# Low parts of the key tiles copied in turns of their own, and the last products all on VectorE: a two-layer decoder trunk on one Trainium2 core

## The chip, the cores and the metric

The kernel runs on one core of one Trainium2 chip. The metric is the device time of one execution in microseconds (us); the time of a kernel is the median over runs. TensorE does the matrix products; VectorE (DVE), ScalarE (ACT) and GpSimd (POOL) do elementwise work; SyncE (SP) issues the loads and stores. PE, DVE, ACT, POOL and SP are the names in the rows.

## The reference

Two layers of a decoder trunk run for 1024 prompt positions and for 8 samples of one position each, with shared weights. Cut to what matters here:

```
# layer 0: gated DeltaNet heads and an RG-LRU beside them -> out projection -> residual
# layer 1: sliding-window attention (16 query heads, 4 key heads of 64, window 128) -> out projection -> residual
# each layer: RMSNorm -> SwiGLU FFN (2816) -> residual; one RMSNorm at the end
def window_attend(qg, kk, vv, rel, keep, sinks, slopes):
    s = einsum('bqhgd,bkhd->bhgqk', qg, kk) * SWA_HEAD_DIM ** -0.5
    s = where(keep, s - slopes * rel, -inf)
    m = maximum(max(s, -1), sink)
    p = exp(s - m)
    p = p / (sum(p, -1) + exp(sink - m))
    return einsum('bhgqk,bkhd->bqhgd', p, vv)
...
y = rmsnorm(x, norm_final)        # x * rsqrt(mean(x*x)) * w, the last thing computed
```

## The kernel before

Activations are kept transposed, the model's channels on the 128 partitions, the positions along a row; the 1024 prompt positions and the 8 samples are cut into two halves of 512 and 520 columns (`t` = 0, 1). Every product with a weight is made of three products of rounded numbers: a value is split into a high part (rounded) and a low part (value less high part); `wh` and `wl` are the two parts of a weight tile, loaded to `raw`, rounded on ACT and subtracted on DVE.

Attention of layer 1: a key tile `k` holds two key heads (p = 0, 1), one on partitions 0 to 63, one on 64 to 127. `ev_k` takes the projected keys out of PSUM and starts the coroutine `co_k(p, t, k)`. For the scores each head's keys must lie on both partition halves. So `co_k` makes, for each half s: the high part in its own half (ACT, in `stack`), the low part by a subtraction (POOL), and the copy of each to the other half (ACT). The four tiles `kf[p]` are the high parts of the two heads (0 and 1) and their low parts (2 and 3). Of (p0, t0) these are s_12462, s_12463, s_12464, s_12465, of (p1, t0) s_12780, s_12781, s_12782, s_12783, in this order. `ready.add(("kf", p, t))` then lets the attention groups `co_att(j, t, q)` start that need it: scores (128x256 products), masked maximum on DVE, exponentials on ACT, scalings on DVE and POOL (`TENSOR_SCALAR s<-s,mx`), transposes on PE through PSUM (`MATMUL PS<-con,s` of 128x128), their evacuation on ACT (`COPY s<-PS`), products with the values (PV, `att_pv`). All this is side work. The main work is the stream of weight products: q, k and v projections, then the output projection (out1), half by half. PSUM is cut into main banks for the weight products and a ring of four side banks (`sd()`) that transposes, scores and PV products take in turn. The eight samples have an attention of their own, `co_att_s`, whose cached keys are loaded while out1 runs. `ev_out` empties out1's banks on DVE and makes the squares for the next norm; `co_blocks` computes that norm from sums of squares on PE.

The order on every engine is fixed when the program is built. The class `Sched` keeps a clock for each engine with estimated costs; each call goes through `Sched.call` (line 237, which is why all rows show L237), and side work is a list of generators that the planner runs between the main products when it believes that they can go on. In a generator `yield "ACT"` means "go on when ACT is believed free", `yield 0` "go on when what I issued is believed done", `yield` of a function "go on when it is true".

`co_final` closes the kernel: for each of three column pieces (432, 344, 256 wide) it computes the final norm's factor `r` and multiplies eight tiles by it, two per output tile, then issues the store. In the last piece (`last`) the eight products are spread over two engines.

Of the kernel before, what the change touches and what calls it, by code (L numbers as in the profile page):

```python
# [321 lines left out]
def trunk_kernel(ctx: ExitStack, tc: tile.TileContext, xT, consts, small, wba, win, lruw, wout0, wqkv, wout1, wgu, wdn,  # L322
# [10 lines left out]
    V, A, G, T, SP, SPA = (S.wrap(n, e) for n, e in (  # L333
        ("DVE", nc.vector), ("ACT", nc.scalar), ("POOL", nc.gpsimd), ("PE", nc.tensor), ("SP", nc.sync),
        ("SPA", nc.scalar)))
# [24 lines left out]
    def alloc(dt=F32):  # L360
        wait_free()
        t, i = new_slot(dt)
        return Buf(t, i, None, dt)
# [12 lines left out]
    def free(*bs):  # L376
        for b in bs:
            if b.half is None:
                free_slots.append(b.slot)
                continue  # L380
            halves[b.dt].append(b)
            owner[b.slot] += 1
            if owner[b.slot] == 2:
                halves[b.dt][:] = [x for x in halves[b.dt] if x.slot != b.slot]
                free_slots.append(b.slot)
# [60 lines left out]
    def split(ap, n):  # L446
        return ap.rearrange("p (c n) -> p c n", c=n)
# [298 lines left out]
    with tc.manual_schedule():  # L746
# [703 lines left out]
        for t in range(2):  # L1450
            gx = half_x(xs0, t)
            for n, w in enumerate((ORDER_0, ORDER_1)[t].split()):
                i = int(w[1])
# [176 lines left out]
        def ffn(layer, wn, dst, sqs, final):  # L1630
# [178 lines left out]
            def ev_last(m, o, w):  # L1809
                def e(ps, full):  # L1810
                    xt = xr[m].a[:, o:o + w]
                    V.tensor_tensor(out=xt, in0=ps[:, 0], in1=xt, op=ALU.add)
                    if m == 0:
                        fin[o] = tuple(halloc().a[:, 0:w] for _ in range(4))
                    q, q7, r, tmp = fin[o]
                    if m < 7:
                        sum_sq(xt, q, m, tmp, G)
                    else:
                        A.activation(out=q7, in_=xt, func=AF.Square)
                        S.spawn(co_final(o, w, [q, q7], r), 0)[0] = S.ready([q, q7], False)  # L1820
                    A.activation(out=xt, in_=xt, func=AF.Identity, scale=sv("nfin", m, 1))
                return e

            def co_final(o, w, qs, r):
                yield from co_norm(qs, w, r, True)
                last = o + w == W
                for m0 in range(0, 8, 2):
                    yb = alloc()
                    y = split(yb.a[:, 0:2 * w], 2)
                    if not last:  # L1830
                        yield "DVE"
                    for i in range(2):
                        (G if last and m0 + i in (3, 5, 7) else V).tensor_tensor(
                            out=y[:, i], in0=xr[m0 + i].a[:, o:o + w], in1=r, op=ALU.mult)
                    SP.dma_start(out=yT.rearrange("(m p) n -> p m n", m=8)[:, m0:m0 + 2, o:o + w], in_=y)
                    free(yb)
# [67 lines left out]
        def ev_k(p, t):  # L1904
            w = HWS[t]

            def f(ps, full):
                k = halloc()
                V.tensor_tensor(out=split(k.a[:, 0:w], 1 + t), in0=ps, in1=rhalf(t), op=ALU.mult)
                if t:  # L1910
                    SP.dma_start(out=p_kT[p * 128:p * 128 + 128, :], in_=k.a[:, 384:512])
                    G.tensor_copy(out=KN[:, 8 * p:8 * p + 8], in_=k.a[:, 512:520])
                else:
                    kf[p] = tuple(alloc(F32R) for _ in range(4))
                S.spawn(co_k(p, t, k), 0)
            return f

        def stack(src, dst, w, o=0):
            for s in range(2):
                a, b = (slice(64 * x, 64 * x + 64) for x in (s, 1 - s))  # L1920
                A.copy(out=dst[s].a[a, o:o + w], in_=src.a[a, 0:w])
                yield a, b, dst[s].a, src.a[a, 0:w], dst[s].a[a, o:o + w].bitcast(F32)

        def co_k(p, t, k):
            cols = slice(512 * t, 512 * t + 512)
            yield "ACT"
            for s, (a, b, hi, x, xh) in enumerate(stack(k, kf[p], 512, 512 * t)):
                kl = kf[p][2 + s].a
                G.tensor_tensor(out=kl[a, cols], in0=x, in1=xh, op=ALU.subtract)
                A.copy(out=hi[b, cols], in_=hi[a, cols].bitcast(F32))  # L1930
                A.copy(out=kl[b, cols], in_=kl[a, cols].bitcast(F32))
            ready.add(("kf", p, t))
            yield 0
            free(k)
# [363 lines left out]
        a, b = ph_in[1][:2]  # L2298
# [177 lines left out]
```

## Time and profile before

| | us |
|---|---|
| median of 3 runs | 2346.76 |
| the runs | 2352.08, 2346.25, 2346.76 |
| the profiled execution | 2351.13 |
| its span, first to last instruction | 2349.0 |
| TensorE busy | 2280.2 (97%) |
| VectorE, ScalarE, GpSimd busy | 1354.2, 989.1, 804.6 |
| mean granted clock of TensorE | 0.986 |

The profiled execution's own time is 2.1 us over its span. The busy times are of one execution; TensorE's clock has the levels 2.4 and 1.2 GHz (1.0 and 0.5 in the windows).

### The profile page before, as it was taken

What the parts mean: (1) busy time and instruction counts of PE and PEld (TensorE: products, weight loads), DVE (VectorE), ACT (ScalarE), POOL (GpSimd) and SP (SyncE); (2) the same over time, 40 slices, a digit from 0 to 9 for tenths busy, and PEclk for the clock granted to TensorE, in tenths of its full rate; (3) what the DMA queues carried; (4) which work ended last, traced back from release to release, by engine and by line L of the source; (5) the groups of instructions that cost most, each with busy time, mean ns of one, the idle gap of its engine ahead of it and who ended that gap; (6) DMA issues with size and microseconds to landing.
All of it is one profiled execution on the core that took longest, in us unless ns stands there. A gap on an engine that the chain in (4) does not pass through costs nothing.

```text
span 2349.0 us, 40227 instructions
## 1 busy us (share of the span) xinstructions
PE 2280.2 (97%) x15984; PEld 2121.2 (90%) x15984; DVE 1354.2 (58%) x2295; ACT 989.1 (42%) x2014; POOL 804.6 (34%) x748
## 2 busy tenths in 40 slices
PE   8899999899999999999999999899999999999998
PEld 6777999689899999999999798779899999999998
DVE  7887687566766665463236557565766544462334
ACT  6775676534522222241124677653522222241214
POOL 1533453332355554410002444431445544410003
PEclk9999999999999999999999999999999999999999
DMA  4332124234334432263213211444333222263222
GB/s 160 103 128 54 51 79 124 75 113 140 126 117 143 128 114 77 81 234 127 70 61 113 64 57 57 130 136 134 132 113 140 90 82 75 79 244 110 71 64 73
DMA packets 122236, 250.69 MB, mean 107 GB/s; under 512 B 24560, under 2 KB 50976, under 8 KB 122016
## 3 DMA queue, kind: packets, MB, share of 16 engines
q1 hardware_dynamic: 121760, 247.83, 32.1%
q8 instruction: 126, 2.06, 0.4%
q14 instruction: 62, 0.51, 0.1%
q10 hardware_dynamic: 288, 0.29, 0.0%
HBM read 199.26 MB, written 50.90 MB: 106 GB/s over the span
## 4 chain that ended last, share of the span: by engine, by line
PE 85%; DVE 6%; ACT 3%; issue 2%; POOL 1%; DMA 1%; SPq 0%; DVEq 0%; ACTq 0%; POOLq 0%
PE PS L237 85%; DVE s L237 4%; ACT s L237 2%; DVE wl L237 1%; POOL s L237 1%; ACT wh L237 1%; SPq L237 0%; ACT L237 0%; DMA s<-ckT 0%; DVE oss L237 0%; DMA pd<-s 0%; DMA s<-xT 0%; DMA lw<-lruw 0%; DMA d<-cm 0%; DVE mx L237 0%
## 5 line engine op out<-in xcount | busy, mean ns | idle before, releaser
L237 PE MATMUL PS<-s,wh 128*128 128x260 f32 (+4 forms) x7936 | 1597.4, 317 | 11.9 <-ACT s L237 6.8
L237 PEld LDWEIGHTS PS<-s,wh 128*128 128x128 f32 x7936 | 1225.0, 189 | 84.2 <-ACT s L237 8.6
L237 PE MATMUL PS<-s,wl 128*128 128x260 f32 (+4 forms) x3968 | 974.6, 317 | 1.6 <-DVE wl L237 1.5
L237 PEld LDWEIGHTS PS<-s,wl 128*128 128x128 f32 x3968 | 658.2, 190 | 34.8 <-DVE wl L237 2.0
L237 POOL TENSOR_TENSOR s<-s,s 128x520 f32<-128x520 f32 (+6 forms) x219 | 296.8, 1356 | 983.7 <-ACT s L237 908.8
L237 DVE TENSOR_TENSOR s<-PS,s 128x520 f32<-128x520 f32 (+7 forms) x430 | 294.0, 684 | 300.6 <-PE PS L237 294.4
L237 DVE TENSOR_TENSOR wl<-raw,wh 128x512 fp32r<-128x512 f32 (+1 forms) x327 | 272.8, 840 | 296.2 <-ACT wh L237 294.2
L237 ACT CAST wh<-raw 128x512 fp32r<-128x512 f32 x352 | 211.7, 608 | 367.6 <-PE PS L237 341.8
L237 PE MATMUL PS<-s,s 128*128 128x260 f32 (+12 forms) x2944 | 343.2, 288 | 9.3 <-ACT s L237 3.3
L237 PEld LDWEIGHTS PS<-s,s 128*128 128x128 f32 (+3 forms) x2944 | 302.4, 171 | 44.4 <-issue 17.0
L237 DVE TENSOR_TENSOR wl<-s,wh 128x512 fp32r<-128x512 f32 x208 | 194.4, 936 | 207.1 <-ACT wh L237 206.8
L237 ACT ACTIVATE s<-s 128x520 f32<-128x520 f32 (+5 forms) x197 | 123.0, 631 | 244.0 <-DVE s L237 232.0
L237 ACT CAST wh<-s 128x512 fp32r<-128x512 f32 x208 | 127.8, 617 | 213.8 <-POOL s L237 109.4
L237 ACT COPY s<-PS 128x512 f32<-128x512 f32 (+6 forms) x296 | 130.9, 469 | 204.9 <-PE PS L237 183.8
L237 DVE TENSOR_TENSOR s<-s,s 128x520 fp32r<-128x520 f32 (+7 forms) x188 | 166.5, 908 | 46.7 <-ACT s L237 45.0
L237 ACT CAST s<-s 128x520 fp32r<-128x520 f32 (+4 forms) x202 | 141.0, 710 | 99.8 <-DVE s L237 48.5
L237 DVE SCALAR_TENSOR_TENSOR s<-s,smt,s 128x512 f32<-128x512 f32 (+3 forms) x160 | 129.5, 834 | 23.8 <-ACT s L237 22.1
L237 PE MATMUL PS<-con,s 128*128 128x128 f32 (+2 forms) x659 | 96.7, 279 | 32.7 <-DVE s L237 15.9
L237 PEld LDWEIGHTS PS<-con,s 128*128 128x128 f32 (+1 forms) x659 | 81.6, 164 | 44.6 <-DVE s L237 17.4
L237 POOL TENSOR_SCALAR s<-s,mx 128x256 f32<-128x256 f32 x64 | 64.3, 1016 | 109.4 <-ACT s L237 62.6
L237 POOL TENSOR_TENSOR s<-s,con 64x256 f32<-64x256 f32 (+1 forms) x56 | 64.1, 1145 | 89.3 <-ACT s L237 51.7
L237 POOL TENSOR_TENSOR s<-raw 128x512 f32<-128x512 f32 x42 | 55.2, 1315 | 85.9 <-DMA hd<-s 40.8
(176 smaller groups left out, 1185.8 us busy)
## 6 DMA issues: line engine op xcount, KB each, us to landing
raw<-wgu SPq DMA_DIRECT2D x94, 512.0 KB, 3.7
raw<-win SPq DMA_DIRECT2D x47, 512.0 KB, 3.6
s<-hd SPq DMA_DIRECT2D x44, 516.0 KB, 5.6
raw<-wout SPq DMA_DIRECT2D x26, 512.0 KB, 3.6
raw<-wdn SPq DMA_DIRECT2D x24, 512.0 KB, 3.7
raw<-wqkv SPq DMA_DIRECT2D x24, 512.0 KB, 3.5
hd<-s SPq DMA_DIRECT2D x44, 260.0 KB, 2.0
hd<-s SPq DMA_DIRECT2D x44, 256.0 KB, 2.0
```

The source lines that it names most:

```text
L237: return sched.call(eng, op, lambda: f(*a, **kw), a, kw)
```

## The change

Two edits. In `co_final` the three products of the last piece that were GpSimd's (m = 3, 5, 7) go to VectorE, which then has all eight. In `co_k` the loop over the two halves now only makes the high parts, their copies and the subtractions; the two copies of low parts follow in a loop of their own, each as a turn that the planner places after the subtraction's believed end and when ACT is believed free. The tile is announced (`ready.add`) after both.

```diff
--- before.py
+++ after.py
@@ -1830,7 +1830,7 @@
                     for i in range(2):
-                        (G if last and m0 + i in (3, 5, 7) else V).tensor_tensor(
+                        V.tensor_tensor(
                             out=y[:, i], in0=xr[m0 + i].a[:, o:o + w], in1=r, op=ALU.mult)
@@ -1924,10 +1924,15 @@
         def co_k(p, t, k):
             cols = slice(512 * t, 512 * t + 512)
             yield "ACT"
+            kls = []
             for s, (a, b, hi, x, xh) in enumerate(stack(k, kf[p], 512, 512 * t)):
                 kl = kf[p][2 + s].a
+                kls.append((kl, a, b))
                 G.tensor_tensor(out=kl[a, cols], in0=x, in1=xh, op=ALU.subtract)
                 A.copy(out=hi[b, cols], in_=hi[a, cols].bitcast(F32))
+            for kl, a, b in kls:
+                yield 0
+                yield "ACT"
                 A.copy(out=kl[b, cols], in_=kl[a, cols].bitcast(F32))
             ready.add(("kf", p, t))
             yield 0
```

ACT's queue around the key tile (p1, t0), at about 1323 us of the trace of before: a piece of the difference of the two orders (- before, + changed). s_12778 is the tile with the projected keys, s_12591 and s_12623 are softmax tiles of attention groups whose transposes come out of PSUM.

```order
 L237 CAST s_12780<-s_12778 64x512
 L237 CAST s_12780<-s_12780 64x512
-L237 CAST s_12782<-s_12782 64x512
 L237 CAST s_12781<-s_12778 64x512
 L237 CAST s_12781<-s_12781 64x512
-L237 CAST s_12783<-s_12783 64x512
 L237 CAST wh<-raw_12788 128x512
 L237 COPY s_12591<-PS 128x384 x2
 L237 COPY s_12851<-PS 128x512
 L237 COPY s_12623<-PS 128x384 x2
```

The two copies of low parts stood between the high parts of the two halves and ahead of the weights' cast; both have left this place. The same queue further on, of the changed kernel alone:

```order
L237 COPY s_12755<-PS 128x512 x2
L237 COPY s_12526<-PS 128x256 x2
L237 CAST s_12782<-s_12782 64x512
L237 CAST s_13007<-s_12526 128x512
L237 COPY s_12778<-PS 128x384
L237 COPY s_12794<-PS 128x384
L237 CAST s_13018<-s_12526 128x512
L237 CAST wh<-raw_12856 128x512
L237 COPY s_12649<-PS 128x256
L237 CAST s_12783<-s_12783 64x512
```

Here the copies stand now, behind the evacuations of later transposes, some ten rows behind their old place.

TensorE's queue at the turn of out1 from its first half to its second, at about 1576 us, of before. s_14327 and s_15175 are inputs of out1 (attention outputs), of the first and second half; s_15477 and s_14815 hold squares and their sum, s_14089 a softmax tile.

```order
L237 MATMUL PS<-s_14327,wh 128x512 x2
L237 MATMUL PS<-s_14327,wl 128x512
L237 MATMUL PS<-s_15175,wh 128x260 x4
L237 MATMUL PS<-s_15175,wl 128x260 x2
L237 MATMUL PS<-s_15175,wh 128x260 x4
L237 MATMUL PS<-s_15175,wl 128x260 x2
L237 MATMUL PS<-s_15178,wh 128x260
L237 MATMUL PS<-con,s_14089 128x128 x4
L237 MATMUL PS<-con,s_14815 128x128 x4
```

And of the changed kernel, where s_14429 is the last input of the first half, s_15206 the first of the second, s_12649 and s_14802 softmax tiles (the second shares its slot with the sum of squares) and s_15340 squares:

```order
L237 MATMUL PS<-s_14429,wh 128x512 x2
L237 MATMUL PS<-s_14429,wl 128x512
L237 MATMUL PS<-con,s_12649 128x128 x4
L237 MATMUL PS<-con,s_14802 128x128 x4
L237 MATMUL PS<-con,s_14802 128x1
L237 MATMUL PS<-con,s_15340 128x1
...
L237 MATMUL PS<-s_14802,s_12851 64x128
L237 MATMUL PS<-s_15206,wh 128x260 x4
L237 MATMUL PS<-s_15206,wl 128x260 x2
```

Before, products of the second half follow those of the first at once; in the changed order transposes, the sums of squares and six PV products stand between them. VectorE's last rows, of the changed kernel:

```order
L237 TENSOR_TENSOR s_22683<-s_20566,s_22525 128x256
L237 TENSOR_TENSOR s_22683<-s_20568,s_22525 128x256
L237 TENSOR_TENSOR s_22687<-s_20686,s_22525 128x256
L237 TENSOR_TENSOR s_22687<-s_20788,s_22525 128x256
L237 TENSOR_TENSOR s_22691<-s_20875,s_22525 128x256
L237 TENSOR_TENSOR s_22691<-s_20960,s_22525 128x256
L237 TENSOR_TENSOR s_22695<-s_21045,s_22525 128x256
L237 TENSOR_TENSOR s_22695<-s_21130,s_22525 128x256
```

Before, five of these eight stand on VectorE and three on GpSimd.

## Rows read from the trace of the kernel before

**Rows 1.** The page's first part: the span, and TensorE's busy time, its share of the span and its instructions.

```profile
span 2349.0 us, 40227 instructions
PE 2280.2 (97%) x15984; PEld 2121.2 (90%) x15984; DVE 1354.2 (58%) x2295; ACT 989.1 (42%) x2014; POOL 804.6 (34%) x748
```

**Rows 2.** Windows: a stretch and its length in us, the busy time and instructions of PE, PEld (weight loads), DVE, ACT and POOL, the granted clock, the share of DMA time, and GB/s.

```profile
1284.00:1600.00 316.00, 301.00 (x2094) 255.88 (x2095) 186.57 (x544) 207.92 (x587) 128.49 (x113) 0.98 0.27 87
1329.00:1334.00 5.00, 0.12 (x2) 0.07 (x2) 0.47 (x1) 3.58 (x7) 1.78 (x2) 0.99 0.00 0
1334.00:1337.30 3.30, 3.30 (x14) 2.76 (x16) 1.23 (x6) 1.99 (x6) 0.00 (x0) 0.50 0.00 0
1345.00:1480.00 135.00, 133.69 (x1085) 121.82 (x1085) 84.34 (x257) 99.65 (x285) 60.29 (x54) 1.00 0.19 56
1579.70:1589.90 10.20, 10.20 (x53) 9.47 (x51) 0.66 (x3) 2.13 (x4) 1.04 (x1) 0.50 0.63 208
```

**Rows 3.** ScalarE's waits from 1276 to 1500 us: what it waited for, us in total, times, the longest.

```profile
ACT s L237 <- POOL s L237: 13.9, 8, 4.7
```

**Rows 4.** The timeline from 1322 to 1337 us: start, duration, engine, operation, in brackets the idle time before and what ended it. GpSimd, ScalarE and TensorE in turn.

```profile
1322.00 6.28 POOL L237 TENSOR_SCALAR s<-s,mx 128x256 f32<-128x256 f32 x6 [6.48 <-ACT s L237]
1328.26 1.26 POOL L237 TENSOR_TENSOR s<-s,s 64x512 fp32r<-64x512 f32 x1
...
1323.63 1.27 ACT L237 CAST s<-s 64x512 fp32r<-64x512 f32 x2
1329.55 1.90 ACT L237 CAST s<-s 64x512 fp32r<-64x512 f32 x3 [4.65 <-POOL s L237]
1332.25 0.62 ACT L237 CAST s<-s 64x512 fp32r<-64x512 f32 x1 [0.79 <-POOL s L237]
1332.89 0.62 ACT L237 CAST wh<-raw 128x512 fp32r<-128x512 f32 x1
1333.41 2.10 ACT L237 COPY s<-PS 128x384 f32<-128x384 f32 x5
...
1328.10 0.63 PE L237 MATMUL PS<-s,wh 128*128 128x512 f32 x2
1328.57 0.49 PE L237 MATMUL PS<-con,s 128*128 128x128 f32 x3
1333.94 0.90 PE L237 MATMUL PS<-con,s 128*128 128x128 f32 x3 [4.88 <-ACT s L237]
```

**Rows 5.** The same view at two of the other key tiles: ScalarE at (p0, t1), and ScalarE, GpSimd and TensorE before the first scores of (p0, t0).

```profile
1403.93 1.90 ACT L237 CAST s<-s 64x512 fp32r<-64x512 f32 x3 [4.03 <-POOL s L237]
...
1293.51 1.26 ACT L237 CAST s<-s 64x512 fp32r<-64x512 f32 x2
1294.20 2.65 POOL L237 TENSOR_TENSOR s<-s,s 64x512 fp32r<-64x512 f32 x2 [4.84 <-ACT s L237]
1298.13 1.11 PE L237 MATMUL PS<-s,s 128*128 128x256 f32 x8
```

**Rows 6.** TensorE around the sample's attention (scores of 128*32), and SP's issue of the second load of cached keys.

```profile
1497.56 0.82 SPq L237 DMA_DIRECT2D s<-ckT  x1
...
1500.36 1.56 PE L237 MATMUL PS<-s,s 128*64 128x256 f32 x12 [1.02 <-ACT s L237]
1503.52 0.63 PE L237 MATMUL PS<-con,s 128*128 128x128 f32 x4 [1.01 <-ACT s L237]
1506.10 0.41 PE L237 MATMUL PS<-s,s 128*32 128x128 f32 x2 [1.62 <-DMA s<-ckT]
1514.46 0.66 PE L237 MATMUL PS<-con,s 128*128 128x128 f32 x4 [1.56 <-DVE mx L237]
1515.36 0.63 PE L237 MATMUL PS<-con,s 128*128 128x128 f32 x4 [0.24 <-DVE mx L237]
1516.79 0.44 PE L237 MATMUL PS<-con,s 128*128 128x128 f32 x2 [0.80 <-ACT s L237]
```

**Rows 7.** The turn of out1: VectorE, ScalarE, TensorE.

```profile
1576.11 0.84 DVE L237 TENSOR_SCALAR s<-s,mx 128x256 f32<-128x256 f32 x2
1576.87 0.68 DVE L237 TENSOR_TENSOR wl<-raw,wh 128x512 fp32r<-128x512 f32 x1
1577.47 0.68 DVE L237 TENSOR_TENSOR s<-PS,s 128x512 f32<-128x512 f32 x1
1578.18 0.63 ACT L237 ACTIVATE s<-s 128x512 f32<-128x512 f32 x1 [3.35 <-DVE s L237]
...
1578.30 0.72 PE L237 MATMUL PS<-s,wh 128*128 128x260 f32 x4 [1.99 <-DVE s L237]
1579.22 4.66 PE L237 MATMUL PS<-con,s 128*128 128x128 f32 x24
```

**Rows 8.** The close: the products of two tiles of the piece of 344 columns and the eight of the last piece in the timeline (the first of VectorE's also alone), and the group of VectorE's five with its mean in ns.

```profile
2331.24 0.94 DVE L237 TENSOR_TENSOR s<-s,s 128x344 f32<-128x344 f32 x2
2342.02 3.35 DVE L237 TENSOR_TENSOR s<-s,s 128x256 f32<-128x256 f32 x5 [1.97 <-ACT s L237]
2342.07 2.69 POOL L237 TENSOR_TENSOR s<-s,s 128x256 f32<-128x256 f32 x3 [1.23 <-ACT s L237]
2342.02 0.43 DVE L237 TENSOR_TENSOR s<-s,s 128x256 f32<-128x256 f32 x1 [1.97 <-ACT s L237]
...
L237 DVE TENSOR_TENSOR s<-s,s 128x256 f32<-128x256 f32 x5 | 3.4, 734 | 2.0 <-ACT s L237 2.0
```

## The prediction

> **What bounds the kernel now.** I read the page's first part before anything else: TensorE is busy for 2280.2 of 2349.0 us [rows 1], so a microsecond is saved only where TensorE stands still or runs at its lower clock, and an engine that waits beside it costs nothing. Next the windows by stage. From 1284 to 1600 us, where the attention layer stands and where the order of the work changes, TensorE is busy for 301.00 of 316 us [rows 2], so at most 15.0 us of standing still can be won there. The reader should see how uneven these are: 4.88 us lie in one stretch from 1329 us on, in which the granted clock was full but almost nothing ran; 135 us behind it hold 1.31 us in all; one stall of 1.99 us ends at 1578.30 us [rows 7]. Two stretches were granted 0.50 of the clock, that is 1.2 instead of 2.4 GHz, each soon after a stall: 3.3 us from 1334 on, and 10.2 us from 1579.7 on [rows 2]. Half clock takes twice as long for the same products, so they cost half their length: 1.65 us (1.7 where I use it) and 5.1 us.
>
> The four executions of before shown stand in two pairs, 2346.25 and 2346.76, and 2351.13 (the profiled one) and 2352.08. The pairs are 5.1 apart, which is what the 10.2 us stretch costs. I read it as: the profiled execution has that stretch, the median has not. That is inferred from the size alone. The sum is made against 2351.13 and then carried to the median.
>
> **The stall at 1329 us, which the change aims at.** ScalarE's waits name the culprit: between 1276 and 1500 us it waits for GpSimd eight times, 13.9 us together, once for 4.7 [rows 3]. In time order [rows 4]: GpSimd starts six softmax scalings at 1322.00 that take 6.28 us, and only then, at 1328.26, the subtraction of co_k for the first half of key tile (p1, t0). ScalarE made the two high copies by 1324.90 and came to the copy of the low part, which needs that subtraction: it waits 4.65 us in its queue, and again 0.79 us for the second half. Behind it in the same queue stand the rounding of the next weights and the evacuation of the transposes (the two COPYs of 128x384), which begins after 1333.41. TensorE is then out of a bank of the side ring: it stands after 3 of the 6 next transposes until 1333.94, 4.88 us.
>
> In the changed order the two low copies are gone from this place, and stand some 10 rows later. Then ScalarE does four half-tile casts in a row, 2 x 1.27 = 2.54 from 1323.63 on, to 1326.2; the weights' cast, 0.62, to about 1326.7; and the first evacuation of two COPYs by about 1327.6 (five COPYs took 2.10, so 0.42 each) [rows 4]. TensorE asked for the bank at 1329.06. So the margin is about 1.4 us and the whole **4.88** goes. GpSimd's second subtraction no longer waits for ScalarE's queue and ends at 1328.26 + 2 x 1.26 = 1330.8, ahead of the moved copies, which stand behind evacuations of transposes that come later than that. Nothing else of GpSimd's stands behind it in rows 4. The half clock directly behind should go with the stall: **1.7**. The bound on the other side is that it stays, 0.
>
> **The other three key tiles.** Eight casts of some 0.63 us move in all; none is added, and co_k issues no DMA. The wait of 4.03 that ends at 1403.93 us [rows 5] lies in the stretch where TensorE lost 1.31 us in 135 [rows 2]: hidden, so its removal is worth nothing, and I take the same for the tile (p1, t1), whose waits are shorter. For (p0, t0) the second moved copy now stands directly ahead of the query's casts and pushes them 0.62 back: those start at 1293.51, GpSimd's two subtractions behind them end at 1294.20 + 2.65 = 1296.85, and TensorE's first scores start at 1298.13 [rows 5]. Of 1.28 us of slack 0.66 is left: nothing. Without that cover it would cost at most 0.62.
>
> **What the new order does behind it.** The planner places side work by its own clock, so from about 1337 to 1590 us the attention groups stand elsewhere between the weights' products; the products are the same. In the smooth stretch to 1480 us I take no difference; bounds: its 1.31 us of gaps gone, or twice as large. Two places can be read.
>
> At the sample's attention, TensorE waits 1.02 and 1.01 us for ScalarE and then 1.62 for the second load of the cached keys, which is issued at 1497.56 [rows 6]. In the new order six more PV products and three more weight products, but eight fewer score products, stand between out1's first product and the sample's scores: by the rows 12 PV products took 1.56, two weight products of 128x512 0.63 (0.47 from start to the next start, 0.23 each), eight scores 1.11 [rows 4 to 6], so 0.78 + 0.7 - 1.11 = about **0.4** us more work to cover the same load. SP's queue has the same order, so the load sets the end; the two waits of 1 us only turn into a longer one for it.
>
> At the turn of out1 from its first half to its second (1576.3), before has six products of the second half behind the last one of the first half, and the seventh needs the bank that VectorE is still to empty. VectorE comes late: a weight subtraction, scalings and another subtraction stand ahead, so that the evacuation runs at 1577.47 to 1578.15, and TensorE waits 1.99 us [rows 7]. In the new order eight transposes and the sums of squares follow the last product of the first half, and six PV products stand ahead of the second half. VectorE has the scalings behind the evacuation, not ahead. The sums need the evacuation (0.68) and ScalarE's square (0.63) [rows 7]: about 1.5 us with the hand-overs, of which eight transposes cover about 0.8 (24 took 4.66 at half clock, so 0.1 each at full) [rows 7]. So about 0.7 us of stall, and up to 0.3 where the second half's low part waits on VectorE behind the norm: 1.0 left, **1.0** gained. Bounds: 0 and 1.99.
>
> **The closing products.** VectorE's five ran from 2342.02 for 3.35 us, GpSimd's three beside them for 2.69 [rows 8]. The first, alone, took 0.43, while the mean of the five is 734 ns: something made the others longer while GpSimd ran. Two products of 128x344 in a row with GpSimd idle take 0.94 for the pair, so 0.35 each at 256 columns [rows 8]. Eight alone: 7 x 0.35 + 0.43 = 2.88, a gain of **0.45**; bounds 8 x 0.43 = 3.44 (a loss of 0.1) and 8 x 0.35 = 2.80 (0.55). The Trainium skill, page "SBUF — State Buffer", section "Who interferes with whom", says that a VectorE instruction with two SBUF inputs contends with a GpSimd instruction that reads SBUF; the trace agrees (0.43 against a mean of 0.73), and by the rule too the products moved off GpSimd should cost VectorE less than they seem to.
>
> **Sum.** 4.88 + 1.7 + 0.4 + 1.0 + 0.45 = 8.4: 2351.13 becomes 2342.7 where out1's turn still falls to half clock, and 2337.6 where it does not. I take the second, since the median of before seems to be without it and the stall ahead of it shrinks. Against the median, 9.2 us or 0.39%. About 0.3% of 2346.76, 7.0 us, is what a measurement of this kernel can tell from no change: the borders are 2339.7 and 2353.8.
>
> **Rivals.**
> - *Half clock stays at the turn* (2342.7, within 0.3%). For it: both long stalls of this stage were followed by half clock [rows 2], and the new order still has a stall there. Against: two of the four executions seem to lack it with the longer stall. 0.22.
> - *Another wait takes the place of the one removed.* ScalarE reaches the moved copies while GpSimd is again behind scalings, or TensorE misses a softmax chain in the re-planned stretch, with its gaps doubled (1.31) and no gain at out1: 2346.0 + 1.3 - 4.88 - 0.45 = 2342.0 without a half clock; 2343.7 if the one of 1.7 stays. Against: GpSimd's subtractions are done some microseconds ahead. 0.15.
> - *More comes back.* Stalls at the turn and at the load go wholly (another 1.0 + 1.2), the small gaps too (1.3): 2337.6 - 3.5 = 2334.1, lower by 1.7 for each half-clock stretch further on that happens not to come. 0.10.
> - *Slower.* The key tile is announced only after the moved copies, so attention groups may start later and pile up at the end, with no weight products beside them. One uncovered group costs 1.56 + 0.24 + 0.80 = 2.6 us, as the sample's does [rows 6]. From 2337.6 it takes seven such groups to pass 2353.8 (six give 2353.2). Against: in the new order the groups are still spread, and from about 1595 us on both orders are the same. 0.05.
> - *The change does nothing* is excluded by the order: the copies do stand elsewhere.
>
> **How the numbers follow.** The case of the sum has 0.48, its own range 2335.5 to 2340.5; I put a sixth of it (0.08) above 2339.7. Faster by over 0.3%: 0.40 + 0.10, and 0.04 of the wait's rival where its gaps don't come, 0.54. Slower 0.05, the rest 0.41. The range reaches from the larger gain less two half-clock stretches, 2334.1 - 3.4 = 2330.7 (a corner, cut to 2331.5), to the case where half clock stays and the small gaps double (2342.7 + 1.3 = 2344.0), some room added: 2344.5.
>
> **What would show it.** The changed trace should have no wait of TensorE over 0.5 us between 1325 and 1340 us, and ScalarE's waits for GpSimd there near 0.5 us where they were 13.9; full clock through 1334 us; at out1's turn a stall of about 1 us; the eight closing products of VectorE in about 2.9 us. The prediction is wrong if TensorE still stands for over 2 us near 1329 us, if a new stall over 2 us appears in the re-planned stretch, or if stretches of half clock elsewhere outweigh the stalls.

## The result, and the profile after

The changed kernel takes 2333.97 us (median of 5 runs, 2327.29 to 2337.82), the kernel before 2346.25 in the same comparison (5 runs, 2342.18 to 2352.08). The ratio is 0.9942, with a 95% interval from 0.9922 to 0.9962: faster by 0.58%, 12.3 us between the medians, where 9.2 us were forecast. The time lies in the forecast range (2331.5 to 2344.5), 3.6 us under the forecast value.

The profiled execution took 2337.39 us. The page's first part, to set beside [rows 1]:

```profile
span 2335.6 us, 40228 instructions
PE 2269.9 (97%) x15984; PEld 2112.2 (90%) x15984; DVE 1346.7 (58%) x2298; ACT 991.5 (42%) x2014; POOL 802.8 (34%) x745
```

The span is 13.4 us shorter, but TensorE's busy time fell by 10.3 us although the products are the same 15984: much of the difference is clock, not standing still. So I cut both traces at the same products (counted from the start; both orders agree at these places) and took the windows of each part. The changed kernel, columns as in [rows 2]:

```profile
0.00:698.14 698.14, 656.63 (x4722) 583.80 (x4723) 498.33 (x943) 392.42 (x783) 274.83 (x298) 0.98 0.33 106
698.14:1323.19 625.05, 624.91 (x4256) 602.45 (x4255) 320.69 (x418) 190.46 (x336) 188.38 (x148) 1.00 0.33 113
1323.19:1329.02 5.83, 5.83 (x40) 4.90 (x40) 2.80 (x9) 3.95 (x9) 5.73 (x5) 1.00 0.27 90
1329.02:1590.76 261.74, 250.28 (x1859) 214.64 (x1856) 152.32 (x459) 176.49 (x500) 104.50 (x93) 0.98 0.28 88
1590.76:1738.70 147.94, 143.76 (x968) 131.79 (x966) 98.94 (x121) 61.48 (x111) 57.45 (x59) 1.00 0.40 136
1738.70:2317.64 578.94, 578.94 (x4074) 565.66 (x4072) 264.69 (x330) 159.78 (x263) 166.27 (x138) 1.00 0.30 103
2317.64:2335.60 17.96, 9.55 (x78) 8.94 (x76) 8.87 (x23) 6.95 (x17) 5.61 (x7) 0.82 0.40 138
```

And the three parts of before that answer to the third, fourth and sixth of them:

```profile
1325.15:1337.58 12.43, 7.55 (x40) 6.09 (x40) 3.36 (x13) 5.85 (x13) 5.63 (x5) 0.86 0.14 42
1337.58:1600.03 262.45, 252.44 (x1860) 215.66 (x1857) 156.08 (x456) 172.44 (x495) 104.48 (x93) 0.98 0.27 88
1750.09:2330.02 579.93, 579.93 (x4074) 566.42 (x4073) 263.83 (x330) 159.48 (x263) 166.30 (x138) 1.00 0.30 103
```

Forty products around the old stall take 5.83 instead of 12.43 us, at full clock and without a gap. The long stretch behind them, in which the order changed, is worth only 0.7 us. ScalarE's casts and TensorE at the place of the old stall, and GpSimd (to set beside [rows 4]):

```profile
1321.68 2.56 ACT L237 CAST s<-s 64x512 fp32r<-64x512 f32 x4
1324.26 0.62 ACT L237 CAST wh<-raw 128x512 fp32r<-128x512 f32 x1
1324.79 1.34 ACT L237 COPY s<-PS 128x384 f32<-128x384 f32 x3
...
1326.37 2.63 POOL L237 TENSOR_TENSOR s<-s,s 64x512 fp32r<-64x512 f32 x2
...
1326.61 0.82 PE L237 MATMUL PS<-con,s 128*128 128x128 f32 x6
1327.19 1.19 PE L237 MATMUL PS<-s,s 128*128 128x256 f32 x8
```

The four high casts run through, the weights' cast and the evacuation follow at once, and the six transposes that were cut in the middle are one run. GpSimd makes both subtractions in a row while ScalarE is already elsewhere. From 1274 to 1490 us ScalarE's waits name GpSimd no more, where they summed to 13.9 us [rows 3].

The turn of out1 went the other way. TensorE, VectorE, ScalarE and GpSimd there (beside [rows 7]), and the clock behind it:

```profile
1558.88 1.03 PE L237 MATMUL PS<-con,s 128*128 128x128 f32 x8
1563.59 0.38 PE L237 MATMUL PS<-con,s 128*128 128x1 f32 x2 [3.67 <-POOL s L237]
1566.05 3.15 PE L237 MATMUL PS<-con,s 128*128 128x1 f32 x14 [2.08 <-ACT s L237]
...
1559.01 0.69 DVE L237 TENSOR_TENSOR wl<-raw,wh 128x512 fp32r<-128x512 f32 x1 [1.81 <-ACT wh L237]
1560.78 0.68 DVE L237 TENSOR_TENSOR s<-PS,s 128x512 f32<-128x512 f32 x1
1562.66 2.02 DVE L237 TENSOR_TENSOR wl<-raw,wh 128x512 fp32r<-128x512 f32 x2 [1.20 <-ACT wh L237]
1564.61 0.68 DVE L237 TENSOR_TENSOR s<-PS,s 128x512 f32<-128x512 f32 x1
1561.49 0.63 ACT L237 ACTIVATE s<-s 128x512 f32<-128x512 f32 x1 [2.52 <-DVE s L237]
1562.03 1.12 ACT L237 CAST wh<-raw 128x512 fp32r<-128x512 f32 x2
1565.37 0.63 ACT L237 ACTIVATE s<-s 128x512 f32<-128x512 f32 x1 [2.22 <-issue]
1560.09 1.98 POOL L237 TENSOR_SCALAR s<-s,mx 128x256 f32<-128x256 f32 x2 [5.06 <-DVE mx L237]
1562.27 1.27 POOL L237 TENSOR_TENSOR s<-s,s 128x512 f32<-128x512 f32 x1 [0.20 <-ACT s L237]
...
1564.50:1574.70 10.20, 8.65 (x43) 7.92 (x44) 6.38 (x14) 3.07 (x6) 3.28 (x3) 0.50 0.82 284
```

The sums of squares (128x1) wait twice, 5.75 us in all, where the old order waited 1.99; half clock follows as in the first profile of before, but its first 1.55 us still lie in the second wait (TensorE is busy for 8.65 of the 10.20 us). The last evacuation starts at 1564.61, 5.6 us after the last weight product ended (1559.0): VectorE is held by weight subtractions that wait for ScalarE's casts (`CAST wh<-raw`), and these stand behind a square (`ACTIVATE`) that waits for VectorE's evacuation before.

At the close VectorE's eight products (beside [rows 8]):

```profile
2328.93 0.37 ACT L237 COPY s<-PS 128x256 f32<-128x256 f32 x1 [1.92 <-PE PS L237]
2329.33 2.77 DVE L237 TENSOR_TENSOR s<-s,s 128x256 f32<-128x256 f32 x8 [1.72 <-ACT s L237]
L237 DVE TENSOR_TENSOR s<-s,s 128x256 f32<-128x256 f32 x8 | 2.8, 418 | 1.7 <-ACT s L237 1.7
```

Eight take 2.77 us, with a mean of 418 ns, where five took 3.35 with 734. From the start of ScalarE's copy of the factor (2328.93) to the end of the span it is 6.7 us, before 7.4 (2341.62 to 2349.0).

### The profile page after: what moved, and what is told of

Same layout as the page of the kernel before. It is cut to its first block, busy times and chain, and to the rows that moved or that the text cites. A ratio compares the mean times of both kernels' runs of the same rounds, so it can differ in the third digit from the quotient of the medians.

```text
span 2335.6 us, 40228 instructions
## 1 busy us (share of the span) xinstructions
PE 2269.9 (97%) x15984; PEld 2112.2 (90%) x15984; DVE 1346.7 (58%) x2298; ACT 991.5 (42%) x2014; POOL 802.8 (34%) x745
## 5 line engine op out<-in xcount | busy, mean ns | idle before, releaser
L237 PE MATMUL PS<-s,s 128*128 128x260 f32 (+13 forms) x2944 | 339.4, 287 | 8.5 <-DVE s L237 3.3
L237 ACT COPY s<-PS 128x512 f32<-128x512 f32 (+7 forms) x296 | 131.3, 468 | 205.1 <-PE PS L237 184.9
```

The lines of the kernel that those rows point to most:

```text
L237: return sched.call(eng, op, lambda: f(*a, **kw), a, kw)
```

## The experiments

Times are medians. The kernel before ran beside the others in three groups: 2345.62 us (35 runs) beside the two edits apart, the copies without turns and the square on VectorE; 2344.81 (29 runs) beside the wait taken away, the wait made longer, the norm held back and the second profile of before; 2344.23 (23 runs) beside the second profile of the changed kernel and the last try at the turn.

**The two edits apart.** With the edit in `co_k` alone:

> Only the edit in co_k; the closing products stay on VectorE and GpSimd as before. TensorE's order is that of the changed kernel. Theory: the stall of 4.88 us at 1329 us and the half clock behind it (1.7) go with this edit alone, so no wait of TensorE over 0.5 us from 1325 to 1340 us, and a time about 1 us above the changed kernel's: 2335 us, 0.5% under before. Rival 'the close does more than the tail shows': this kernel is within 0.3% of before (above 2339).

2334.21 us (12 runs), ratio 0.9951 [0.9932, 0.9970]. With the close alone (the first hunk of the diff):

> Only the closing products all on VectorE; co_k as before. Every engine's order up to the last products is that of before. Theory: the eight products take about 2.5 to 2.9 us instead of 3.35, so 0.5 to 1.0 us less than before, which the comparison cannot tell from nothing; the stall of 4.88 us at 1329 stays. Rival: the close gives several us, 2342 or less against 2346 of before.

2344.11 us (12 runs), ratio 0.9995 [0.9976, 1.0015]; the stall of 4.88 us is there. So `co_k` carries the gain. The close is too small for the medians; in its trace the eight products do what they do in the changed kernel, and the end comes 0.7 us sooner after the factor.

**Later, but without turns of their own.** The loop of the changed kernel without its two yields:

```diff
             for kl, a, b in kls:
-                yield 0
-                yield "ACT"
                 A.copy(out=kl[b, cols], in_=kl[a, cols].bitcast(F32))
```

> The closing products as before; in co_k the two low copies follow both halves' parts at once, in the same turn, without turns of their own. TensorE's order is that of before, row for row. Theory: ScalarE still meets the wait for GpSimd, only later: the four high casts end about 1326.2, the first low part is there at 1329.5, the second at 1330.8, so the evacuation comes at about 1332 and TensorE stands for 3 to 3.5 us instead of 4.88; time 1.5 us under before (2344.8). Rival 'the place behind both halves is enough': the stall is gone and the time is near the changed kernel's (2336 or less).

2343.70 us (12 runs), ratio 0.9990 [0.9969, 1.0011]. ScalarE and TensorE:

```profile
1313.44 2.57 ACT L237 CAST s<-s 64x512 fp32r<-64x512 f32 x4
1319.34 0.62 ACT L237 CAST s<-s 64x512 fp32r<-64x512 f32 x1 [3.33 <-POOL s L237]
1320.67 0.62 ACT L237 CAST s<-s 64x512 fp32r<-64x512 f32 x1 [0.72 <-POOL s L237]
1322.36 0.55 PE L237 MATMUL PS<-con,s 128*128 128x128 f32 x3 [3.51 <-ACT s L237]
```

The stall is 3.51 us, at the upper end of what was expected; the 1.9 us of the medians can't be told from nothing. A place behind both halves is not enough, since GpSimd's subtractions, behind its scalings, still come later than that.

**The wait taken away without a new order.** As the last kernel, and for the tile (p1, t0) alone the subtractions run on VectorE while the planner books GpSimd, so that TensorE's order is that of before:

```diff
-                G.tensor_tensor(out=kl[a, cols], in0=x, in1=xh, op=ALU.subtract)
+                if (p, t) == (1, 0):
+                    S.call("POOL", "tensor_tensor", lambda: nc.vector.tensor_tensor(
+                        out=kl[a, cols], in0=x, in1=xh, op=ALU.subtract), (),
+                        dict(out=kl[a, cols], in0=x, in1=xh, op=ALU.subtract))
+                else:
+                    G.tensor_tensor(out=kl[a, cols], in0=x, in1=xh, op=ALU.subtract)
```

> The kernel before with the low copies behind both halves' parts (no turns), and for the key tile (p1, t0) alone the two subtractions on VectorE, with the planner told GpSimd, so that TensorE's and ScalarE's orders stay as they were: the wait goes without any new order of the products. Theory: VectorE is free from about 1326.6 us on, both low parts are there by 1327.9, ScalarE evacuates at about 1329.5, so TensorE's stall of 4.88 us shrinks to 0.5 or less and the half clock behind it goes: 6 us under before (about 2339.5). Rival 'the gain is in the new order of the products': time within 2 us of before (2344 or more), although the stall is gone. Rival 'the stall costs more clock than the stretch behind it shows': 9 us or more under before (2336.5 or less).

2339.22 us (12 runs), 5.6 us under before; ratio 0.9981 [0.9966, 0.9996]. The transposes wait 0.66 us instead of 4.88, and the forty products take 7.05 us at full clock:

```profile
1322.93 0.55 PE L237 MATMUL PS<-con,s 128*128 128x128 f32 x3 [0.66 <-ACT s L237]
...
1318.36:1325.41 7.05, 6.39 (x40) 4.97 (x40) 4.17 (x11) 5.11 (x11) 3.65 (x3) 1.00 0.26 74
```

So the wait for GpSimd makes the stall, and about half of the whole gain comes with it alone. The median is within 0.3 us of the theory's 2339.5 and outside both rivals, but the interval is wide: 0.9 to 8.0 us under before.

**The wait made longer.** In the kernel before, each of the two subtractions of (p1, t0) is done twice on GpSimd, the second time unknown to the planner (one more `nc.gpsimd.tensor_tensor` with the same operands):

> The kernel before with each of the two subtractions of key tile (p1, t0) done twice on GpSimd, the second one not known to the planner; all orders else are those of before. Theory: two more subtractions of 1.26 us stand in the chain, so the stall at 1329 us grows from 4.88 to about 7.4, and the time by 2.5 us and what more half clock behind it costs (0 to 3.4): 2348 to 2352. Rival 'the stall is not on the path': no change.

2347.34 us (12 runs), 2.5 over before and 0.7 short of the expected range, ratio 1.0014 [0.9995, 1.0033]. The medians alone don't settle it; the trace does: the stall is 7.49 us and the forty products take 14.84 us.

```profile
1331.92 0.90 PE L237 MATMUL PS<-con,s 128*128 128x128 f32 x3 [7.49 <-ACT s L237]
...
1320.52:1335.36 14.84, 7.36 (x40) 6.00 (x40) 3.16 (x11) 5.64 (x13) 8.15 (x7) 0.77 0.12 35
```

Of the 2.6 us that the stall grew, 2.2 to 2.4 reach the length of this part (12.43 and 12.66 in the two profiles of before).

**Second profiles of both kernels.** Before:

> The kernel before once more, for a second profile: which gaps and stretches of half clock come again. Theory: the stall of 4.88 us at 1329 us with half clock behind it comes again, the layer-1 FFN takes the same 579.9 us, while half clock elsewhere (layer 0, out1's turn) falls differently. Rival: half clock stands at the same places as in the first profile.

One run, 2352.82 us. The stall is 4.87 us again, the FFN 579.93. But half clock also stood at out1's turn for 10.24 us again, which speaks for the rival there. The changed kernel:

> The changed kernel once more, beside the one that relieves VectorE at the turn, for its time on the same chip and a second profile. Theory: median 2334 within 2, no stall near 1329 us, stalls of 3.67 and about 2 us at out1's turn with half clock for about 10 us, layer 1's FFN 579.0 us. Rival: the half clock at the turn comes in one profile and not in another, as in the kernel before.

2334.31 us (12 runs), 9.9 us under before, ratio 0.9960 [0.9938, 0.9982]: the stalls at the turn 3.66 and 1.88 with 10.24 us of half clock, the FFN 578.92. With the profiles of the kernels above this makes six of the old order and, with the square on VectorE below, four of the changed one, cut at the same products (lengths in us):

| part | old order: before, again, close only, no turns, wait longer, wait gone | changed: after, again, keys only, square on VectorE |
|---|---|---|
| layer 0 to 700 us | 700.1, 700.1, 691.1, 689.9, 695.4, 693.3 | 698.1, 692.3, 698.4, 696.5 |
| the stall's place | 12.4, 12.7, 12.7, 11.2, 14.8, 7.1 | 5.8, 5.8, 5.8, 5.8 |
| re-ordered, to 1600 | 262.5, 263.6, 259.9, 261.3, 257.2, 260.4 | 261.7, 261.2, 261.1, 262.2 |
| 1600 to 1750 | 150.1, 150.5, 148.0, 148.5, 150.7, 149.9 | 147.9, 147.0, 146.8, 147.6 |
| FFN to 2330 | 579.9 in all six | 578.9, 578.9, 579.0, 578.9 |
| the close | 19.0, 19.0, 18.1 (new close), 19.0, 18.7, 19.0 | 18.0, 18.0, 18.7 (old close), 18.0 |

**What holds the turn.** The seventh square added on VectorE instead of GpSimd, in layer 1 of the changed kernel:

```diff
-                    G.tensor_tensor(out=sqs[0].a[:, 0:w], in0=sqs[0].a[:, 0:w], in1=q.a[:, 0:w], op=ALU.add)
+                    (V if layer and m == 6 else G).tensor_tensor(out=sqs[0].a[:, 0:w], in0=sqs[0].a[:, 0:w], in1=q.a[:, 0:w], op=ALU.add)
```

> The changed kernel with one instruction on another engine: in layer 1's out1 the square of the seventh tile (m = 6) is added to the sum on VectorE and not on GpSimd; every order else is that of the changed kernel. It asks what the stalls of 3.67 and 2.08 us at the turn of out1 wait for. Theory: the first sums of squares wait for GpSimd's addition, which stands behind two softmax scalings (1.98 us); on VectorE the first stall shrinks by 1 to 2 us, the sum of both from 5.75 to about 4, and the time by 1 to 2 us, up to 5 more where the half clock of 10.24 us behind it does not come. Rival: the stalls are set by ScalarE's square of the last tile and VectorE's queue, and stay at 5.5 us or more in all.

2333.69 us (12 runs), ratio to before 0.9949 [0.9931, 0.9968], beside 0.9951 of the keys alone: no gain in time. The stalls are 2.99 and 1.93 us, 4.92 in all, between theory and rival: GpSimd's addition was worth only 0.8 us against the first profile of the changed kernel (5.75), 0.6 against the second (5.54).

```profile
1562.86 0.59 PE L237 MATMUL PS<-con,s 128*128 128x1 f32 x2 [2.99 <-DVE s L237]
1565.37 1.87 PE L237 MATMUL PS<-con,s 128*128 128x1 f32 x8 [1.93 <-ACT s L237]
```

The same, and the norm's sums held back by 5 us of the planner's time:

```diff
-                    S.spawn(co_blocks(layer, t, sqs), 0)
+                    S.spawn(co_blocks(layer, t, sqs), 0)[0] += 5000 if layer and t == 0 else 0
```

> The changed kernel with two edits at the turn of out1: the seventh square is added on VectorE, and the planner may start the norm's sums 5 us later, so that PV products, the first products of the second half and transposes stand ahead of the sums of squares. The stalls there were 3.67 + 2.08 us, with half clock for 10.24 us. Theory: some 4 us of products now cover them, 1 to 2 us of stall are left and the half clock does not come: 4 to 9 us under the changed kernel (2325 to 2330). Rival 'the wait only moves': the products ahead of the sums wait for VectorE's low parts or for a bank, the stalls sum to 5 us or more and the time is that of the changed kernel, 2334.

2336.40 us (12 runs), ratio to before 0.9959 [0.9944, 0.9974]. The rival holds: the wait only moves, to the PV products that now stand first, since their transposes' evacuation on ScalarE stands behind the last square.

```profile
1564.29 2.45 PE L237 MATMUL PS<-s,s 128*64 128x256 f32 x12 [6.49 <-ACT s L237]
```

The third try leaves all orders as they are and frees VectorE: the square as above, and the three weight subtractions around the last two evacuations run on GpSimd, booked for VectorE by the planner.

```diff
+        if u in (394, 395, 396):
+            S.call("DVE", "tensor_tensor", lambda: nc.gpsimd.tensor_tensor(
+                out=l[:, 0:n], in0=t, in1=h[:, 0:n].bitcast(F32), op=ALU.subtract), (),
+                dict(out=l[:, 0:n], in0=t, in1=h[:, 0:n].bitcast(F32), op=ALU.subtract))
+        else:
...
```

> The changed kernel, orders of TensorE and ScalarE kept, with VectorE relieved at the turn of out1: the seventh square is added on VectorE, and the three weight subtractions that stand around the last two evacuations go to GpSimd, the planner being told VectorE. Theory: the sums of squares at the turn wait for a chain of VectorE's queue (weight subtractions that wait for ScalarE) and ScalarE's squares; with the queue free the evacuations follow the products at once and the stalls of 3.67 + 2.08 us shrink to 2 or less, the half clock behind them becomes rarer: 4 to 8 us under the changed kernel. Rival 'another engine's wait takes over' (GpSimd's subtractions late for the next products): stalls of 4 us or more in all at the turn, time within 2 us of the changed kernel.

2333.21 us (12 runs), ratio to before 0.9956 [0.9937, 0.9976], beside 2334.31 of the changed kernel. The stalls are what the theory said:

```profile
1560.52 0.38 PE L237 MATMUL PS<-con,s 128*128 128x1 f32 x2 [1.04 <-DVE s L237]
1561.83 2.18 PE L237 MATMUL PS<-con,s 128*128 128x1 f32 x14 [0.93 <-ACT s L237]
...
1327.03:1586.02 258.99, 250.89 (x1860) 214.84 (x1856) 151.95 (x457) 176.44 (x500) 108.41 (x95) 0.98 0.27 89
```

1.97 us in all, and the re-ordered part takes 258.99 us, 2.1 to 3.3 less than in the four profiles of the changed kernel. Half clock behind it still comes, for 6.83 us. The 4 to 8 us in time are not there: the 1.1 us between the medians can't be told from nothing. It is no proven better version, but it settles what the turn waits for.

## Why the prediction was right, and where its steps failed

**The stall at 1329 us: right in place, cause and size.** 4.88 and 1.7 were forecast, 6.6 in all; the part shrank by 6.6 us (12.43 to 5.83), by 6.8 against the other two profiles of the unchanged order. Taking the wait away by itself brought 5.6 us of the median, lengthening it lengthened the part, and moving the copies only a little moved the stall only a little. The price of half clock was right here (TensorE's busy time in this part fell from 7.55 to 5.83 us), but half its length is not always the price: in the second profile of before the half clock was 6.83 us long and the part only 0.23 us longer, because 2.4 us of it lay in the stall and 0.55 behind the part.

**The other key tiles: right.** The wait of 4.03 us went and nothing around it grew shorter by it; no score product of (p0, t0) came late.

**The re-ordered stretch: wrong by the turn of out1.** I expected 1.0 us back there and 1.0 left. The stall grew from 1.99 to 5.75, so one of the prediction's own signs of being wrong, a new stall over 2 us in the re-planned stretch, came true. The step that failed is "VectorE has the scalings behind the evacuation, not ahead": I looked at the rows next to the last evacuation and took it to follow its products at once. The two weight subtractions ahead of it wait for ScalarE's casts, and these stand behind the square of the tile before, which waits for the evacuation before that. The runs at the turn show it: with the addition moved and VectorE's queue freed 3.8 of the 5.75 us went, with the addition alone 0.8.

In the smooth part two new gaps of 0.89 and 1.78 us came, the second for a query's evacuation behind scalings on VectorE; the gaps there sum to 2.9 us, where 1.3 were.

At the sample's attention 0.4 us were forecast and 3.7 came: the six waits of [rows 6] sum to 6.25 us, the two that stand there in the changed order to 2.56. The load's wait is 1.43 us instead of 1.62, about as I had it; that the two waits ahead of it and the three behind the sample's scores would go, with one of 1.13 us in their place, I had not counted. TensorE at the second of the new gaps, then at the load and behind the sample's products:

```profile
1472.17 0.70 PE L237 MATMUL PS<-s,wh 128*128 128x512 f32 x2 [1.78 <-DVE s L237]
...
1493.20 0.41 PE L237 MATMUL PS<-s,s 128*32 128x128 f32 x2 [1.43 <-DMA s<-ckT]
...
1500.73 0.63 PE L237 MATMUL PS<-con,s 128*128 128x128 f32 x4 [1.13 <-ACT s L237]
```

In all TensorE stands for 11.46 us in this stretch, before for 10.01, and is busy for 250.28 us instead of 252.44. Of the 2.2 us less, 0.8 are the half clock that lay in the second wait at the turn. The others are products that ran faster in the new order (12 PV products took 1.09 us at 1497.93 us of the changed kernel, 1.56 in [rows 6]); why was not looked into. So the stretch came out even: 0.7 us shorter instead of 1.4.

**The close: right, slightly too small.** Seven starts of 0.34 us apart and one product: 2.77 where I worked out 2.88. The end came 0.7 us sooner, not 0.45: 0.58 are VectorE's, and SP had issued the last of the four stores 3.6 us after the start of the factor's copy, before 4.4. One reading was not clean: the pair of 128x344 products that I took for free of GpSimd ended at 2332.18 us, and a product of GpSimd's began at 2331.92. VectorE's kept its 0.51 us all the same, so the price holds.

**The step to the median: wrong reasoning.** I read four executions as two pairs 5.1 us apart, one with half clock at the turn, one without. Beside the experiments before ran 87 times, spread from 2335.8 to 2356.6 us with a standard deviation of 5.4 us; there are no two levels. That the old order can go without half clock there is true all the same: of its six profiles, all with a stall of 1.99 or 2.00 us at the turn, only the two of the unedited kernel have it. Three of the other four have 3.41 to 10.24 us of it at the sample's attention; with the longer wait the whole re-ordered stretch ran at full clock:

```profile
1335.36:1592.58 257.22, 247.62 (x1859) 211.25 (x1856) 156.29 (x456) 172.32 (x496) 104.46 (x93) 1.00 0.28 90
```

What failed for the changed kernel is the other reason that I gave, that "the stall ahead of it shrinks": the stall grew, and all four profiles of the changed order have the 10.24 us of half clock at the turn. By my own list this is the rival "half clock stays at the turn", which I had put at 2342.7, within 0.3%.

**What made up for it.** Three things that I had not counted. The part from 1600 to 1750 us is 2.3 us shorter in the mean of the profiles (149.6 to 147.3): in five of the six profiles of the old order half clock stands in it (3.41 or 6.83 us; halved, 2.3 us in the mean of the six), in none of the four changed ones. The FFN behind it is 0.99 us shorter, each time. The close's part is about 1 us shorter, of which 0.7 come behind the factor. With the stall's 6.8, and 0.7 lost in the means of the re-ordered part (260.81 to 261.55), this sums to about 10.3 us; the mean of the 12 later runs of the changed kernel is 10.5 us under that of the 87 of before (10.0 under the 23 beside it). Why half clock no longer stands between 1600 and 1750 us is open: the gaps there are much the same (3.1 to 4.1 us in the old order, 3.4 to 4.2 in the changed one), and the kernel with the norm held back, which has no stall at 1329 us either, has 3.41 us of it there. Layer 0, where nothing changed, differs by up to 10 us between profiles of the old order and 6 us between those of the changed one; the two profiles that were compared first differ there by 1.9 us, which is chance.

So the forecast time was near in part by luck: a loss of 3.8 us at the turn was made up by an uncounted gain at the sample's attention, and a wrong step of 5 us to the median by gains behind the stretch that it had not listed. Its claim that TensorE's stall of 4.88 us and the clock behind it are the core of the change is what the experiments bear out: 6.8 of some 10 us by the traces, 5.6 by the median of the kernel that takes the wait away alone. Of the other gains only what changed in the traces is shown, not why.

## What to carry to other kernels

What counted here was not how long a waiting instruction waits but what stands behind it in its engine's queue: a copy that nobody was waiting for yet held up the evacuation for which TensorE stood. Before forecasting how long a re-planned order waits, follow each instruction ahead of the critical one to what it waits for itself, through both engines, and not only the rows beside it. Where runs of one kernel spread by 5 us, cut the traces at the same products and compare part by part; a single profile against a single profile would have credited 2 us of layer 0's chance to the change.

## What the runs showed of the hardware

**The same products, in the same order, took 1 us less in the FFN.** 4074 products took 579.92 to 579.94 us in six profiles of the old order and 578.92 to 578.96 in those of the changed one, at full clock and without a gap; the kernel with the norm held back took 579.84. Blocks of 200 products repeat within 0.002 us from run to run of one order, and differ by up to 0.17 us between orders. TensorE's, VectorE's, ScalarE's and GpSimd's rows there are the same by operation, name and shape. The buffers that the tiles sit in may differ; whether they do it was not tried, and the cause is open.

**VectorE's products beside GpSimd's took 0.94 or 0.95 us instead of 0.42**, three of the five of the old close. GpSimd's three took 0.90 to 0.97, where one alone took 0.73 (at 2330.11 us of before). So five of VectorE's beside three of GpSimd's took longer (3.35 us) than all eight on VectorE alone (2.77).

**The spread of the runs goes with the granted clock.** Over the 87 runs of before, time and mean granted clock correlate with -0.95. The quickest (2335.79 us) had a mean granted clock of 0.990, the slowest (2356.61) 0.982; the difference, 0.8% of the time, is 19 of the 21 us between them. Half clock that fell into a stall cost nothing: with the longer wait the clock fell at 1328.01 us, for 6.83 us, while TensorE stood until 1331.92; the forty products kept TensorE busy for 7.36 us, against 7.55 behind the shorter wait with 3.41 us of half clock.
